# A decoder layer's down-projection: 23 instead of 20 pairs of row blocks in seven products, and second-half weight sums made by accumulating DMAs

## The chip, the cores and the metric

The kernel runs on one core of one Trainium2 chip. The metric is the device time of one execution in microseconds (us), lower is better. The kernel before took 1053.34 us (median of three runs, 1053.02 to 1053.57).

The engines of the core are named as in the profile: PE is TensorE (matmuls; PEld is its weight load), DVE is VectorE, ACT is ScalarE, POOL is GpSimd, SP is the engine that issues nearly all DMAs here. SPq and POOLq are the sequencers that issue them.

## The reference

A hybrid decoder layer on 256 tokens of width 2048, float32 throughout: an input projection, two groups of attention heads, an output projection, and a gated MLP with a causal convolution. The change lies in the MLP:

```python
h = rmsnorm(x, pre_ffn_g[l])
u = causal_dwconv(h @ w_up[l], conv_w[l], conv_b[l])      # w_up: 2048 x 11264
gate, val = jnp.split(u, 2, axis=-1)
y = (jax.nn.gelu(gate, approximate=True) * val) @ w_down[l]   # w_down: 5632 x 2048
x = x + rmsnorm(y, post_ffn_g[l])
```

## The kernel before

**Three matmuls for one.** A float32 product is made from two parts of each operand, a high part rounded to float32r and the remainder (low): high by high, high by low, low by high. For each weight tile ACT writes the high part (`act.copy`, CAST in the profile) and DVE subtracts it from the loaded tile to get the low part (TENSOR_TENSOR). Both parts stand in one of five buffers `wpair`; the loaded tile stands in one of five buffers `raw` of 1024 columns (512 KB). DVE's subtraction is the last reader of a `raw` buffer, and SP may load that buffer again after it; PE's last matmul frees a `wpair`.

**The order of the work.** PE's instructions stand in program order. Those of the other engines are ordered by a scheduler, apart from some that `keep_in_program_order` pins. A counter `tick()` runs once per weight unit of a projection (8 per projection of the MLP, 16 per pair of gate and value projections); `later(n, f)` calls `f` after n such steps.

**The MLP in two halves.** Each half of the 5632 hidden channels is done in two stages. In the `w_up` stage (lines 1002 to 1049) eleven groups `g` of 256 channels each take a gate projection and a value projection (`proj_S`, matmuls of 256 columns on line 300); DVE, ACT and for some sums POOL then make the convolution, the gelu, the product, and the split tiles `G`. In the `w_down` stage (lines 1161 to 1207) the 22 row blocks of that half, taken as 11 pairs, are multiplied by `w_down`, for `n` = 0 and then 2: each time two column blocks of 512 for both blocks of 128 tokens (matmuls of 512 columns on line 1072).

**Four products or seven.** A pair of row blocks against two column blocks is a 2 by 2 block product: eight block products, three matmuls each. `four` does four of them (12 matmuls), for one column block. `seven` does the whole pair in seven products (21 matmuls instead of 24) by a Strassen-Winograd scheme. It needs sums of activation blocks (tiles `s`, `sums`, made by POOL in the `w_up` stage on lines 1030 to 1033, then split by ACT and DVE) and four sums of weight blocks. The weight sums come from one of two places:
- made in the `w_down` stage, by four DVE operations of 512 columns on the loaded tiles (line 1105; the second tile is then called `low`);
- stored beforehand: in the `w_up` stage SP loads the weight blocks (`staged`, line 922), DVE makes the sums (line 928, four operations of 256 columns, twice per pair), SP stores them to DRAM (`t_dram`, line 931). In the `w_down` stage they are loaded as two tiles of 512 KB, the second of them called `two`.

Either way a pair in `seven` splits 3.5 tiles of 1024 columns, and a pair in two calls of `four` splits 2.

`SEVENS` says, for each half and each `n`, at which step `i` of the loop on line 1168 a pair's seven products stand; `STORED` says which pairs' sums are stored beforehand. Each step `i` also holds the products of one pair by `four`: `n` and `n + 1`, except in the last stage (second half, `n` = 2), where `n + 1` comes later. The first half has 6 and 6 pairs in seven products, the second half 5 and 3. After the last seven of an `n`, `fold` (line 1139) adds four PSUM banks into `y_sb`; after the last `four`, `down` (line 1059) adds the other banks.

Buffers that the change touches: `yy` (two of 1024 columns, holding the convolved projections in the `w_up` stage and `low` in the `w_down` stage), `gb0` (one, for `staged` of the second half, for `two`, and later for the gain of the last norm), `gb1` (one, for those activation sums that don't fit in `sums`, named `more`, and later for the gain), `u0` to `u2` (three, the scaled projections ahead of the convolution).

Of the kernel before, what the change touches and what calls it, by code (L numbers as in the profile page):

```python
# [8 lines left out]
F32 = mybir.dt.float32  # L9
# [18 lines left out]
SEVENS = (((0, 0, 1, 1, 2, 2), (0, 0, 1, 1, 2, 2)), ((0, 0, 1, 1, 2), (0, 1, 2)))  # L28
STORED = (((0, 0, 1), (0, 0, 3), (0, 0, 5), (0, 2, 1), (0, 2, 3), (0, 2, 5), (1, 0, 1)), ((1, 0, 3), (1, 2, 0), (1, 2, 1), (1, 2, 2)))
# [5 lines left out]
def hybrid_layer(ctx: ExitStack, tc: tile.TileContext, x, pre_mix_g, w_in, b_forget, sinks,  # L35
# [367 lines left out]


# [448 lines left out]
    with tc.tile_pool(name="ffn", bufs=1) as fp:  # L853
# [22 lines left out]
        NU = 3  # L876
# [3 lines left out]
        fp.tile([P, 8], F32, tag="gap", name="gap")  # L880
# [26 lines left out]
        in_dram = {}  # L907

        def stage(half, n, u, start, step, room):

            k = half * FHALF + u * 2
            t = in_dram[half, n, u] = tc.dram_tile([P, 4, 512], F32, name="t_dram")
            src = w_down[k * P:(k + 2) * P, n * 512:(n + 2) * 512].rearrange(
                "(a p) (b c) -> p a b c", p=P, b=2)
            for i, j in enumerate((slice(0, 256), slice(256, 512))):
# [8 lines left out]
                def add(b=b):  # L924
                    b11, b12, b21, b22 = (b[0][:, i, :] for i in range(4))
                    for y, p, q in ((b11, b12, b11), (b12, b22, b12), (b22, b22, b11),
                                    (b21, b21, b22)):
                        tc.keep_in_program_order(dve.tensor_tensor(y, p, q, op=ALU.subtract))
# [49 lines left out]
        for half in range(2):  # L978
# [5 lines left out]

            def sums_at(u):
                w, at = 384 if u < least else 512, 768 * min(u, least) + 1024 * max(u - least, 0)
                if not u:
                    sums.append(main.tile([P, 4096], F32R, tag="x", name="sums"))
                if at + 2 * w <= 4096:
                    x = sums[0][:, at:at + 2 * w]  # L990
                else:
                    x = fp.tile([P, UNIT], F32R, tag="gb1", name="more")[:, 0:2 * w]
                sums.append((x[:, :w], x[:, w:]))
                return w, *sums[-1]

            for g in range(FHALF // 2):
# [24 lines left out]
                if g < most:  # L1021
# [9 lines left out]
                    pool.tensor_tensor(s1, a21, a22, op=ALU.add)  # L1031
                    pool.tensor_tensor(s2, s1, a11, op=ALU.subtract)
                    pool.tensor_tensor(s4, a12, s2, op=ALU.subtract)
# [6 lines left out]
                if not g:  # L1040
                    if half:
                        room = lambda: fp.tile([P, 4, 256], F32, tag="gb0", name="staged")
                    else:
                        four_of = main.tile([P, 4, 4, 256], F32, tag="y", name="staged")
                        rooms = [four_of[:, i] for i in range(4)]
                        room = lambda: rooms.append(rooms[0]) or rooms.pop(0)
# [37 lines left out]
            def seven(n, u, last, banks, opened):  # L1084
# [8 lines left out]
                else:  # L1093
# [3 lines left out]
                    [x[:, i * P:i * P + P] for x in sums[1 + u]] if i < 3 or u >= least  # L1097
                    else parts_of(u * 2, 1) for i in range(4)]
                (w11,) = split_into(w_parts(UNIT, held=False), top, 1)
                w21, w22 = split_into(w_parts(UNIT, held=False), low, 2)  # L1100
                if t is None:
                    b11, b12, b21, b22 = (x[:, i:i + 512] for x in (top, low) for i in (0, 512))
                    for y, p, q in ((b11, b12, b11), (b12, b22, b12), (b22, b22, b11),
                                    (b21, b21, b22)):
                        made = dve.tensor_tensor(y, p, q, op=ALU.subtract)
# [201 lines left out]
```

## Time and profile before

| | |
|---|---|
| median of three runs | 1053.34 us |
| the profiled execution's own time | 1053.3 us |
| its span, first to last instruction | 1051.4 us |
| mean granted TensorE clock | 0.997 |
| first `w_up` stage of the MLP | about 340 to 577 us of the span |
| first `w_down` stage | 577 to 688.5 us |
| second `w_up` stage | 688.5 to 928 us |
| second `w_down` stage | 928 to about 1044 us |

The page of the profile gives the busy time of each engine and the chain of work that ended last. Matmuls are pipelined and their ends are modelled, so the mean duration of a matmul in a group is longer than its share of the time; its pace is read from the chain, which puts runs of matmuls together. Busy time of an engine that PE doesn't wait for is not time of the kernel.

### The profile page before, as it was taken

To read this page: it belongs to the slowest core of one execution; us is meant where nothing else is said; L and a number is where in the kernel's file an instruction comes from. 1 tells how busy PE (TensorE), PEld (TensorE's weight loads), DVE (VectorE), ACT (ScalarE), POOL (GpSimd) and SP (SyncE) were. 2 spreads that over 40 slices of the span, in tenths; PEclk is the share of its full clock that TensorE was granted. 3 is DMA by queue.
4 is the path that set the end of the run, shared out by engine and by line. 5 is a ranking of instruction groups with operands and counts; after the bars stand their busy time and mean duration, and the time that the engine had idled before them with its cause. 6 is when DMAs were issued, how large, how long until landed. Compare 5 with 4: busy or idle time off the path is not lost.

```text
span 1051.4 us, 19021 instructions
## 1 busy us (share of the span) xinstructions
PE 1040.0 (99%) x7240; PEld 958.0 (91%) x7240; DVE 837.2 (80%) x1365; ACT 626.9 (60%) x1025; POOL 166.5 (16%) x210
## 2 busy tenths in 40 slices
PE   9999999999999999999999999999999999999996
PEld 7899988888888999999999888899999999988886
DVE  5999877887467888888877988967788777799783
ACT  6777757667557655555555655645565455566561
POOL 3253245441122210100000000000111000000023
PEclk9999999999999999999999999999999999999998
DMA  8645557555874878888875886777677776767783
GB/s 292 199 129 168 182 159 214 164 180 171 294 248 153 255 252 294 287 264 273 283 232 170 263 269 226 244 233 239 220 235 246 226 244 219 236 216 246 244 306 115
DMA packets 187335, 238.98 MB, mean 227 GB/s; under 512 B 8268, under 2 KB 154988, under 8 KB 186348
## 3 DMA queue, kind: packets, MB, share of 16 engines
q1 hardware_dynamic: 186924, 237.37, 69.5%
q8 instruction: 57, 0.93, 0.3%
q10 hardware_dynamic: 320, 0.40, 0.1%
q14 instruction: 34, 0.28, 0.1%
HBM read 221.86 MB, written 15.75 MB: 226 GB/s over the span
## 4 chain that ended last, share of the span: by engine, by line
PE 90%; DVE 4%; ACT 2%; DMA 1%; POOL 1%; issue 1%; SPq 0%; DVEq 0%; POOLq 0%; ACTq 0%
PE bank_att L300 23%; PE bank_acc L300 21%; PE bank_acc L1072 15%; PE bank_acc L317 12%; PE bank_acc L263 5%; PE bank_att L1072 5%; PE bank_acc L270 3%; DVE wpair L122 1%; PE bank_att L317 1%; POOL scr L450 1%; PE bank_att L518 1%; DMA raw<-in_w_in_dram 1%; PE bank_att L483 1%; PE bank_att L527 1%; DMA x_in<-in_x_dram 1%
## 5 line engine op out<-in xcount | busy, mean ns | idle before, releaser
L122 DVE TENSOR_TENSOR wpair<-raw,wpair 128x1024 fp32r<-128x1024 f32 (+3 forms) x317 | 383.6, 1225 | 116.9 <-ACT wpair L119 115.8
L119 ACT CAST wpair<-raw 128x1024 fp32r<-128x1024 f32 (+3 forms) x316 | 320.3, 1032 | 155.6 <-issue 62.6
L300 PE MATMUL bank_att<-hT,wpair 128*128 128x256 f32 x2112 | 241.2, 276 | 0.0
L300 PEld LDWEIGHTS bank_att<-hT,wpair 128*128 128x128 f32 x2112 | 240.4, 188 | 0.2
L300 PE MATMUL bank_acc<-hT,wpair 128*128 128x256 f32 x1920 | 219.2, 276 | 0.0
L300 PEld LDWEIGHTS bank_acc<-hT,wpair 128*128 128x128 f32 x1920 | 218.3, 188 | 0.0
L1072 PE MATMUL bank_acc<-wpair,G 128*128 128x512 f32 x636 | 153.5, 389 | 0.0
L1072 PEld LDWEIGHTS bank_acc<-wpair,G 128*128 128x128 f32 x636 | 119.1, 188 | 24.5
L263 PE MATMUL bank_acc<-hT,wpair 128*128 128x512 f32 x384 | 94.9, 394 | 0.0
L263 PEld LDWEIGHTS bank_acc<-hT,wpair 128*128 128x128 f32 x384 | 69.5, 188 | 13.2
L317 PE MATMUL bank_acc<-wpair,oT 128*128 128x512 f32 x336 | 78.0, 391 | 0.0
L317 PEld LDWEIGHTS bank_acc<-wpair,oT 128*128 128x128 f32 x336 | 62.6, 188 | 12.8
L1030 POOL TENSOR_TENSOR s<-yy 128x128 f32<-128x128 f32 x11 | 7.5, 681 | 408.1 <-DVE yy L1019 408.1
L320 ACT CAST wpair<-raw 128x1024 fp32r<-128x1024 f32 (+1 forms) x54 | 48.0, 892 | 36.2 <-PE bank_acc L1072 17.6
L321 DVE TENSOR_TENSOR wpair<-raw,wpair 128x1024 fp32r<-128x1024 f32 (+1 forms) x54 | 55.0, 1023 | 14.3 <-ACT wpair L320 13.4
L899 ACT ACTIVATE yy<-u,cw 128x256 f32<-128x256 f32 x88 | 48.4, 596 | 20.4 <-DVE u L894 15.3
L270 PE MATMUL bank_acc<-hT,wpair 128*128 128x256 f32 x384 | 49.4, 280 | 0.0
L270 PEld LDWEIGHTS bank_acc<-hT,wpair 128*128 128x128 f32 x384 | 47.4, 188 | 1.4
L317 PE MATMUL bank_acc<-wpair,hT 128*128 128x384 f32 (+1 forms) x288 | 47.7, 321 | 0.0
L317 PEld LDWEIGHTS bank_acc<-wpair,hT 128*128 128x128 f32 x288 | 45.4, 188 | 0.1
L320 ACT CAST G<-yy 128x256 fp32r<-128x256 f32 x44 | 16.0, 406 | 46.8 <-POOL yy L1031 23.9
L901 DVE SCALAR_TENSOR_TENSOR yy<-u,cw,yy 128x256 f32<-128x256 f32 x88 | 39.1, 482 | 2.4 <-ACT yy L899 2.2
(253 smaller groups left out, 1204.9 us busy)
## 6 DMA issues: line engine op xcount, KB each, us to landing
raw<-in_w_up_dram SPq DMA_DIRECT2D x176, 512.0 KB, 4.6
raw<-in_w_down_dram SPq DMA_DIRECT2D x68, 512.0 KB, 5.1
raw<-in_w_in_dram SPq DMA_DIRECT2D x51, 512.0 KB, 5.3
raw<-in_w_out_dram SPq DMA_DIRECT2D x32, 512.0 KB, 4.1
staged<-in_w_down_dram SPq DMA_DIRECT2D x44, 256.0 KB, 5.5
t_dram<-staged SPq DMA_DIRECT2D x22, 512.0 KB, 3.2
raw<-t_dram SPq DMA_DIRECT2D x14, 512.0 KB, 3.7
raw<-in_w_in_dram SPq DMA_DIRECT2D x16, 384.0 KB, 3.4
```

The lines of the kernel that those rows point to most:

```text
L119: i1 = act.copy(hi[:, cs], raw[:, cs])
L122: i2 = dve.tensor_tensor(lo[:, cs], raw[:, cs], hi[:, cs].bitcast(F32), op=ALU.subtract)
L263: pe.matmul(b, hi[:, a, m * P:(m + 1) * P], hT[:, kt, 0:512], start=(kt == 0), stop=(last == (0, kt)))
L270: pe.matmul(b[:, 256:512], lo[:, a, m * P:(m + 1) * P], hT[:, u * 4 + a, 0:256], start=False, stop=(last == (1, u * 4 + a)))
L300: pe.matmul(b[:, m * 256:(m + 1) * 256], ws[:, a, m * P:(m + 1) * P], hT[:, kt, i * 256:(i + 1) * 256], start=not begun, stop=last == (low ...
L317: pe.matmul(b, a, r[:, cols], start=(first and i == 0), stop=(last and i == 2))
L320: act.copy(hi, src)
L321: dve.tensor_tensor(lo, src, hi.bitcast(F32), op=ALU.subtract)
L450: pool.tensor_tensor(dst, dst, row, op=ALU.mult)
L899: act.activation(y, u[:, 2:258], AF.Identity, bias=cw[:, 3, ch:ch + 1], scale=cw[:, 2, ch:ch + 1])
L901: dve.scalar_tensor_tensor(y, u[:, 1:257], cw[:, 1, ch:ch + 1], y, op0=ALU.mult, op1=ALU.add)
L1072: pe.matmul(b, x, r, start=b not in opened and not i, stop=closes and i == 2)
```

## The change

The change does seven things:
- `SEVENS`: 7, 7, 6 and 3 pairs in seven products instead of 6, 6, 5 and 3. In the first half the last step that holds sevens (`i` = 2) now holds three of them. In the second half, `n` = 0, it still holds two, and there is one step less.
- `MADE`: in the first `w_up` stage the sums of ten pairs of the first half are made and stored by way of SBUF, where seven pairs were done (one of those seven was of the second half). A half pair now takes 7 steps instead of 10, so that all take 140 steps as before.
- The scheme's signs are turned so that the weight sums need additions alone. In `stage` three DVE operations (one of 512 columns, two of 256) replace four of 256.
- `ADDED`: the seven stored pairs of the second half are no longer made by DVE. SP copies the blocks from DRAM to DRAM (two DMAs of 512 KB), and POOL issues three DMAs that add in place (512, 256 and 256 KB), each 14 steps after the one before; the pairs start 16 steps apart.
- The second tile of stored rows, `two`, is loaded into the two `yy` buffers, not into the one buffer `gb0`.
- Activation sums that don't fit go to `gb1` and `gb2`; `gb2` is new.
- Two buffers `u` instead of three, and `cs` and `last` share the buffer of `s`.

```diff
-SEVENS = (((0, 0, 1, 1, 2, 2), (0, 0, 1, 1, 2, 2)), ((0, 0, 1, 1, 2), (0, 1, 2)))
-STORED = (((0, 0, 1), (0, 0, 3), (0, 0, 5), (0, 2, 1), (0, 2, 3), (0, 2, 5), (1, 0, 1)), ((1, 0, 3), (1, 2, 0), (1, 2, 1), (1, 2, 2)))
+SEVENS = (((0, 0, 1, 1, 2, 2, 2), (0, 0, 1, 1, 2, 2, 2)), ((0, 0, 1, 1, 2, 2), (0, 1, 2)))
+MADE = tuple((0, n, u) for n in (0, 2) for u in (0, 1, 3, 5, 6))
+ADDED = tuple((1, 0, u) for u in (1, 3, 4, 5)) + tuple((1, 2, u) for u in range(3))
...
+        def added(at, start):
+
+            t = in_dram[at] = tc.dram_tile([P, 4, 512], F32, name="t_dram")
+            src = corners(*at)
+
+            def copy():
+                for a in range(2):
+                    tc.keep_in_program_order(sp.dma_start(t[:, 2 * a:2 * a + 2, :], src[:, a]))
+
+            def add(to, what):
+                return lambda: tc.keep_in_program_order(
+                    pool.dma_start(to, what, accum_op=ALU.add))
+
+            for d, f in enumerate((copy, add(t[:, 0:2, :], src[:, :, 1, :]),
+                                   add(t[:, 3, :], t[:, 0, :]), add(t[:, 2, :], t[:, 3, :]))):
+                later(start + d * 14, f)
...
-        NU = 3
+        NU = 2
...
-                    c = fp.tile([P, 256], F32, tag="cs", bufs=1, name="cs")
+                    c = fp.tile([P, 512], F32, tag="s", name="cs")[:, 0:256]
...
                 def add(b=b):
-                    b11, b12, b21, b22 = (b[0][:, i, :] for i in range(4))
-                    for y, p, q in ((b11, b12, b11), (b12, b22, b12), (b22, b22, b11),
-                                    (b21, b21, b22)):
-                        tc.keep_in_program_order(dve.tensor_tensor(y, p, q, op=ALU.subtract))
+                    x = b[0]
+                    for y, p, q in ((x[:, 0:2], x[:, 0:2], x[:, 1:4:2]),
+                                    (x[:, 3], x[:, 3], x[:, 0]), (x[:, 2], x[:, 2], x[:, 3])):
+                        tc.keep_in_program_order(dve.tensor_tensor(y, p, q, op=ALU.add))
...
-                if at + 2 * w <= 4096:
-                    x = sums[0][:, at:at + 2 * w]
+                if sum(x.shape[1] for x in sums) + n > 4096:
+                    x = fp.tile([P, UNIT], F32R, tag=f"gb{len(places)}", name="more")
...
-                    for at in STORED[half]:
-                        start = stage(*at, start, 19 if half else 10, room)
+                    for at in MADE:
+                        start = stage(at, start, 7, lambda: rooms.append(rooms[0]) or rooms.pop(0))
+                if half and not g:
+                    for i, at in enumerate(ADDED):
+                        added(at, 1 + i * 16)
...
-                        own = None if tail else fp.tile([P, UNIT], F32, tag="gb0", name="two")
+                        own = None if tail else fp.tile([P, UNIT], F32, tag="yy", bufs=2, name="two")
```

How instructions move, at three places. First, VectorE at the end of the first half's `n` = 0. Before, from the last pair in sevens to the last `down` (`wpair` rows are splits, L1145 to L1148 the fold, L1061 `down`; names after the arrow are inputs):

```order
L321 TENSOR_TENSOR wpair<-two,wpair 128x1024
L122 TENSOR_TENSOR wpair<-raw,wpair 128x1024 x3
L1145 TENSOR_TENSOR y_sb<-bank_att,y_sb 128x512
L122 TENSOR_TENSOR wpair<-raw,wpair 128x1024
L1146 TENSOR_TENSOR y_sb<-bank_att,y_sb 128x512
L1147 TENSOR_TENSOR y_sb<-bank_att,y_sb 128x512
L321 TENSOR_TENSOR wpair<-raw,wpair 128x512
L1148 TENSOR_TENSOR y_sb<-bank_att,y_sb 128x512
L321 TENSOR_TENSOR wpair<-low,wpair 128x1024
L122 TENSOR_TENSOR wpair<-raw,wpair 128x1024
L1061 TENSOR_TENSOR y_sb<-bank_acc,y_sb 128x512 x2
```

The same place in the changed kernel (L1174 to L1177 are the fold, L1090 is `down`):

```order
L322 TENSOR_TENSOR wpair<-two,wpair 128x1024
L123 TENSOR_TENSOR wpair<-raw,wpair 128x1024 x2
L322 TENSOR_TENSOR wpair<-raw,wpair 128x512
L1174 TENSOR_TENSOR y_sb<-bank_att,y_sb 128x512
L322 TENSOR_TENSOR wpair<-raw,wpair 128x1024
L1175 TENSOR_TENSOR y_sb<-bank_att,y_sb 128x512
L1176 TENSOR_TENSOR y_sb<-bank_att,y_sb 128x512
L1090 TENSOR_TENSOR y_sb<-bank_acc,y_sb 128x512
L1177 TENSOR_TENSOR y_sb<-bank_att,y_sb 128x512
L123 TENSOR_TENSOR wpair<-raw,wpair 128x1024
L1090 TENSOR_TENSOR y_sb<-bank_acc,y_sb 128x512 x3
```

One pair by `four` less stands between the sevens and the next `n`, so that the fold and all of `down` come within two splits of each other.

Second, SyncE's queue at the same place, from the last two pairs in sevens on. Before (`raw` of 512 columns and of 1024 columns are a stored pair's untouched blocks, `two` and `raw<-t_dram` its sums):

```order
L74 DMA raw<-in_w_down_dram 128x512
L74 DMA raw<-in_w_down_dram 128x1024
L74 DMA two<-t_dram 128x1024
L74 DMA raw<-t_dram 128x1024
L74 DMA raw<-in_w_down_dram 128x2x512 x2
L74 DMA low<-in_w_down_dram 128x1024
L74 DMA raw<-in_w_down_dram 128x2x512 x2
```

In the changed kernel:

```order
L75 DMA raw<-in_w_down_dram 128x512
L75 DMA raw<-in_w_down_dram 128x1024
L75 DMA two<-t_dram 128x1024
L75 DMA raw<-t_dram 128x1024
L75 DMA raw<-in_w_down_dram 128x512
L75 DMA raw<-in_w_down_dram 128x1024
L75 DMA two<-t_dram 128x1024
L75 DMA raw<-t_dram 128x1024
L75 DMA raw<-in_w_down_dram 128x2x512 x2
```

Two stored pairs now follow each other, where one was followed by loads for `four`.

Third, GpSimd's queue in the second `w_up` stage, at its third and fourth group. Before it held only the activation sums:

```order
L1030 TENSOR_TENSOR s<-yy 128x128
L1031 TENSOR_TENSOR yy<-yy 128x128
L1032 TENSOR_TENSOR s<-yy 128x128
L1033 TENSOR_TENSOR s<-yy,s 128x128
L1030 TENSOR_TENSOR s<-yy 128x128
L1031 TENSOR_TENSOR s<-yy 128x128
L1032 TENSOR_TENSOR s<-s,yy 128x128
```

In the changed kernel the adding DMAs stand between them:

```order
L1060 TENSOR_TENSOR s<-yy 128x128
L1061 TENSOR_TENSOR yy<-yy 128x128
L1062 TENSOR_TENSOR s<-yy 128x128
L1063 TENSOR_TENSOR s<-yy,s 128x128
L424 DMA t_dram<-t_dram 128x512 x2
L424 DMA t_dram<-in_w_down_dram 128x2x512
L1060 TENSOR_TENSOR s<-yy 128x128
```

From the fourth group on, a group's four sums stand behind three adding DMAs of three different pairs.

More of the change, by code (lines that the diff above doesn't have):

```diff
@@ L402, in hybrid_layer, with corners @@
             unit_T(parts, u, bq0)
+        in_dram = {}
+        def corners(half, n, u):
+            k = half * FHALF + u * 2
+            return w_down[k * P:(k + 2) * P, n * 512:(n + 2) * 512].rearrange(
+                "(a p) (b c) -> p a b c", p=P, b=2)
+        def added(at, start):
[10 more added lines that the diff above has]
+                later(start + d * 14, f)
         gst = const.tile([32, P], F32, tag="gpre", name="gst")
@@ L879, in hybrid_layer @@
             pool.memset(u[:, :, 0:2], 0.0)
-        fp.tile([P, 8], F32, tag="gap", name="gap")
+        fp.tile([P, 16], F32, tag="gap", name="gap")
         cnt = [0]
@@ L905, in conv, with stage @@
             return y
[L907 to L914, printed above, removed]
+        def stage(at, start, step, room):
+            t = in_dram[at] = tc.dram_tile([P, 4, 512], F32, name="t_dram")
+            src = corners(*at)
             for i, j in enumerate((slice(0, 256), slice(256, 512))):
@@ L983, in hybrid_layer, with sums_of @@
             sums = []
+            places = []
             def sums_at(u):
-                w, at = 384 if u < least else 512, 768 * min(u, least) + 1024 * max(u - least, 0)
+                n = 768 if u < least else 1024
                 if not u:
-                    sums.append(main.tile([P, 4096], F32R, tag="x", name="sums"))
-                if at + 2 * w <= 4096:
-                    x = sums[0][:, at:at + 2 * w]
-                else:
-                    x = fp.tile([P, UNIT], F32R, tag="gb1", name="more")[:, 0:2 * w]
-                sums.append((x[:, :w], x[:, w:]))
-                return w, *sums[-1]
+                    places.append(main.tile([P, 4096], F32R, tag="x", name="sums"))
+                if sum(x.shape[1] for x in sums) + n > 4096:
+                    x = fp.tile([P, UNIT], F32R, tag=f"gb{len(places)}", name="more")
+                    places.append(x)
+                    x = x[:, 0:n]
+                else:
+                    at = sum(x.shape[1] for x in sums)
+                    x = places[0][:, at:at + n]
+                sums.append(x)
+                return n // 2, x[:, :n // 2], x[:, n // 2:]
+            def sums_of(u, i):
+                w = sums[u].shape[1] // 2
+                return [sums[u][:, j * w + i * P:j * w + i * P + P] for j in range(2)]
             for g in range(FHALF // 2):
@@ L1039, in hybrid_layer @@
                     split(*parts, s[:, :w])
[L1040 to L1046, printed above, removed]
-                    start = 0
-                    for at in STORED[half]:
-                        start = stage(*at, start, 19 if half else 10, room)
+                if not half and not g:
+                    four_of = main.tile([P, 4, 4, 256], F32, tag="y", name="staged")
+                    rooms = [four_of[:, i] for i in range(4)]
+                    start = 0
+                    for at in MADE:
[3 more added lines that the diff above has]
+                        added(at, 1 + i * 16)
             if half == 1:
@@ L1096, in seven @@
                 s2, s3, s4, s1 = [
-                    [x[:, i * P:i * P + P] for x in sums[1 + u]] if i < 3 or u >= least
-                    else parts_of(u * 2, 1) for i in range(4)]
+                    sums_of(u, i) if i < 3 or u >= least else parts_of(u * 2, 1)
+                    for i in range(4)]
                 (w11,) = split_into(w_parts(UNIT, held=False), top, 1)
@@ L1102, in seven @@
                     b11, b12, b21, b22 = (x[:, i:i + 512] for x in (top, low) for i in (0, 512))
-                    for y, p, q in ((b11, b12, b11), (b12, b22, b12), (b22, b22, b11),
+                    for y, p, q in ((b11, b11, b12), (b12, b12, b22), (b22, b22, b11),
                                     (b21, b21, b22)):
-                        made = dve.tensor_tensor(y, p, q, op=ALU.subtract)
+                        made = dve.tensor_tensor(y, p, q, op=ALU.add)
                         if n and not u and y is b11:
@@ L1264, in hybrid_layer @@
             finish(0, slice(n * 512, (n + 1) * 512), r, sp)
-        last = fp.tile([P, 256], F32, tag="cs", bufs=1, name="last")
+        last = fp.tile([P, 512], F32, tag="s", name="last")[:, 0:256]
         for h in range(2):
```

12 lines of the change are left out of this document (6 added, 6 removed).

## Prediction

> **What bounds the kernel now.** I read the page first, then the chain that ended last, then stretches of the stages that the change touches.
>
> ```profile
> span 1051.4 us, 19021 instructions
> PE 1040.0 (99%) x7240; PEld 958.0 (91%) x7240; DVE 837.2 (80%) x1365; ACT 626.9 (60%) x1025; POOL 166.5 (16%) x210
> PE 90%; DVE 4%; ACT 2%; DMA 1%; POOL 1%; issue 1%; SPq 0%; DVEq 0%; POOLq 0%; ACTq 0%
> ```
>
> The profiled execution took 1053.3 us, 1.9 us around its span of 1051.4; it lies 0.04 us from the median of 1053.34. I sum against 1053.3. PE holds 90% of the chain, and the question is whether it ever pauses where the change works. The chain, in order of time (start, duration, instructions):
>
> ```profile
> 359.35 21.79 PE bank_att L300 x192
> 381.14 21.76 PE bank_acc L300 x192
> ...
> 555.22 21.76 PE bank_acc L300 x192
> ...
> 607.60 6.80 PE bank_acc L1072 x30
> 614.40 2.04 PE bank_att L1072 x9
> ...
> 621.20 11.56 PE bank_acc L1072 x51
> ...
> 1034.48 8.64 PE bank_att L317 x72
> 1044.55 0.75 DVE y_sb L1233
> ```
>
> Each run of 192 matmuls of 256 columns takes 21.76 us, 113.3 ns each, and the next begins where it ends. In `w_down` 30 matmuls of 512 columns take 6.80 us, 9 take 2.04, 51 take 11.56: always 226.7 ns. From 359 to 1043 us PE has no gap to speak of. So the change can gain only by the matmuls that it removes, and loses whatever makes PE wait. DVE, DMA and POOL matter only as suppliers. The same by stretches (busy us of PE, PEld, DVE, ACT, POOL with counts, then PE clock, DMA share, GB/s):
>
> ```profile
> 381.10:402.90 21.80, 21.80 (x195) 21.80 (x194) 19.42 (x33) 12.02 (x17) 2.43 (x4) 1.00 0.96 305
> 389.00:409.00 20.00, 20.00 (x179) 20.00 (x178) 17.25 (x28) 11.61 (x17) 1.24 (x3) 1.00 1.00 332
> 486.00:496.00 10.00, 10.00 (x90) 10.00 (x89) 8.92 (x16) 5.71 (x9) 0.00 (x0) 1.00 1.07 372
> 577.00:632.80 55.80, 55.80 (x247) 46.19 (x247) 50.11 (x59) 34.84 (x39) 0.00 (x0) 1.00 0.80 266
> 753.80:775.50 21.70, 21.70 (x194) 21.70 (x193) 17.53 (x28) 12.21 (x17) 2.03 (x4) 1.00 0.70 221
> ```
>
> PE stays busy even where the DMA share is 1.00 over 20 us at 332 GB/s, and 1.07 over 10 us at 372.
>
> **The matmuls removed.** A pair by seven is 7 x 3 = 21 matmuls of 512 columns, by `four` twice 24. The first half goes from 6 x 21 + 5 x 24 = 246 (246 x 0.2267 = 55.8 us, the stretch 577.0 to 632.8) to 7 x 21 + 4 x 24 = 243, for each of two `n`. The second half's `n` = 0 goes from 5 x 21 + 6 x 24 = 249 to 246; the last stage keeps its 3. Nine matmuls go: 9 x 0.2267 = **2.04 us**. Everything else is off PE.
>
> **VectorE in the first `w_up` stage.** Group rows (line, form, count; busy, mean ns), then one tile's operations (min/median/max ns):
>
> ```profile
> L928 DVE TENSOR_TENSOR staged<-staged 128x256 f32<-128x256 f32 x88 | 37.8, 430 | 1.6
> L321 DVE TENSOR_TENSOR wpair<-low,wpair 128x1024 fp32r<-128x1024 f32 x18 | 22.0, 1221 | 1.3 <-ACT wpair L320 0.9
> L1061 DVE TENSOR_TENSOR y_sb<-bank_acc,y_sb 128x512 f32<-128x512 f32 x15 | 9.7, 682 | 6.4 <-PE bank_acc L1072 6.4
> L1105 DVE TENSOR_TENSOR low<-low x9: 681/686/695, 576.0 to 959.9; 128x512 f32<-128x512 f32 x9
> ```
>
> Seven pairs cost 7 x 8 x 0.430 = 24.1 us. Ten cost 10 x 2 x (0.686 + 2 x 0.430) = 30.9 us, +6.8 us over 140 steps of 1.36 us (21.76 / 16). In a stretch of 21.8 us that is 3.5 us for 2.8, so DVE at its busiest goes from 19.42 to some 20.2 of 21.8. It is hidden by the 2.4 us of idle time there; without that cover it would be PE's loss, at most 0.8 us a group. Counted at nothing. The second `w_up` stage loses 32 x 0.430 = 13.8 us of DVE, which PE doesn't wait for.
>
> **DMA in the first `w_up` stage.** Issues by line (count, KB each, us to landing):
>
> ```profile
> raw<-in_w_up_dram SPq DMA_DIRECT2D x176, 512.0 KB, 4.6
> staged<-in_w_down_dram SPq DMA_DIRECT2D x44, 256.0 KB, 5.5
> t_dram<-staged SPq DMA_DIRECT2D x22, 512.0 KB, 3.2
> two<-t_dram SPq DMA_DIRECT2D x8, 512.0 KB, 6.2
> ```
>
> Eight loads of `w_up` in 21.76 us are 193 GB/s. The 11 stored pairs take 44 loads and 22 stores, so one moves 1 MB in and 1 MB out, 2.1 MB: seven in 190 us are 77 GB/s, ten are 110. The stretch at 305 GB/s would ask for 338, a mean one for 303 to 312. Held against 332 over 20 us and 372 over 10 us with PE unbroken, it passes, with landings later than 4.6 us. The cover is five `raw` buffers of 2.72 us each (24 matmuls), 13.6 us. If 332 were a hard limit, the densest group would lose 338 / 332, 0.4 us. Counted at nothing.
>
> **The `w_down` stages.** For the first half's last two steps of an `n` (three sevens, two pairs by `four`, the fold, `down`) PE has 111 matmuls, 25.2 us. DVE has 3 x (0.68 + 3 x 1.22) = 13.0 for sevens, 4 x 1.22 = 4.9 for `four`, 4 x 0.69 = 2.7 for the one pair made in place, 4 x 0.68 for the fold and as much for `down`: 26.1 us, 0.9 more than PE. Before, the last three steps had 24.2 us in 25.8. But busy times overlap at their ends, as merged rows show (start, duration, count):
>
> ```profile
> 963.42 2.35 DVE L122 TENSOR_TENSOR wpair<-raw,wpair 128x1024 fp32r<-128x1024 f32 x2
> 629.59 1.28 DVE L1061 TENSOR_TENSOR y_sb<-bank_acc,y_sb 128x512 f32<-128x512 f32 x2
> ```
>
> Two splits take 2.35, so they follow at 1.13 us, and two `down` at 0.60. By these the sum is 3 x 4.0 + 4 x 1.13 + 12 x 0.60 = 23.7 us, 1.5 less than PE has. The cost per `n` lies between 0 and 0.9 us; I take 0, since the second reckoning is the one by start times. The earlier steps of an `n` lose two in-place pairs (i = 0 now has none), so DVE enters them less loaded.
>
> SP's queue there:
>
> ```profile
> 616.89 1.23 DVE L321 TENSOR_TENSOR wpair<-two,wpair 128x1024 fp32r<-128x1024 f32 x1
> 618.14 0.34 SPq L74 DMA_DIRECT2D two<-t_dram  x1
> 620.80 1.05 ACT L119 CAST wpair<-raw 128x1024 fp32r<-128x1024 f32 x1 [1.16 <-DMA raw<-in_w_down_dram]
> ```
>
> With one buffer, `two` waits until DVE has read the one before (618.12), and the `raw` loads queued behind it on SP make ACT wait 1.16 us for one. PE didn't notice, as the chain shows. Two buffers move that wait to the reader of two tiles ago, which takes this stall away; next late are the loads of two stored pairs in a row, 3.5 MB in 9.5 us (42 matmuls), with three `raw` loads per 4.76 us against a landing of 3.2 to 6.2. No gain, no cost.
>
> **POOL and DMA in the second `w_up` stage.** Seven pairs bring 14 SP copies of 512 KB and 21 adds on POOL. The copies wait for nothing. An add waits for the DMA before it in its pair; behind it on POOL stand the next group's activation sums, and for these ACT waits already:
>
> ```profile
> ACT G L320 <- POOL yy L1031: 23.9, 9, 3.5
> POOL s L1030 <- DVE yy L1019: 408.1, 11, 239.0
> ```
>
> POOL is busy 2.03 of 21.7 us in the stretch from 753.8, so it idles some 19 us a group ahead of its sums, and each add was preceded by its source a group (16 steps, 21.76 us) or 14 steps earlier. Landings are 3.2 to 6.2 us, so the waits are over before POOL comes to them: 0. No row shows an adding DMA. A bound from below is a copy of its size (5.5 us, its engines' time at 1 x); from above I take three times that, 17 us, still under 21.76. The adds' data per pair is 1.05 MB, as are the copies', so in a group of 21.76 us they ask 48 + 48 GB/s beside 193, in all 289, less than the first stage. Counted at nothing; nearest are the loads and stores of 3.2 to 6.2 us.
>
> Two `u` buffers: a buffer is written again 21.76 us after its last writing, and its readers follow within a group: 0. The gain's early load, 512 KB, and the shared `cs`: 0.
>
> **Sum.** 1053.3 - 2.04 = **1051.3 us**.
>
> **The rivals.** 0.2% (2.1 us) is about what a measurement of this kernel can tell from no change; the bounds are 1051.2 and 1055.4, and my sum lies 0.1 us inside the first.
>
> *VectorE late at the end of an `n`.* The upper reckoning holds: up to 0.9 us twice in the first half, and the new `raw` pinch as much again: 1051.6 to 1053.3. For it speaks 26.1 against 25.2; against it the start times. 0.18.
>
> *Slower matmuls.* Every `G` tile moves in SBUF, and here matmuls of one shape have two paces:
>
> ```profile
> 355.69 3.66 PE bank_acc L263 x16
> ```
>
> 16 of 512 columns in 3.66 us are 228.8 ns, 2.1 over those of `w_down`. On the 243 + 243 + 246 that remain in the changed parts that would cost 1.5 us: 1052.8. Against it, nothing ties the pace to an address. 0.05.
>
> *Slower: the DMA engines bound the second `w_up` stage.* If an add keeps them k times as long as a copy, they are asked for 193 + 48 + 48k GB/s. From 332, k = 1.9, PE starts to wait; over the 152 us of the seven pairs k = 2.2 makes 347 / 332, +7 us, and 1058; k = 3 makes +24. For it: adds read two sources. Against it: 372 GB/s over 10 us, and a slow queue would delay itself before it delays `raw`, whose cover is 13.6 us. 0.10. The Trainium skill ("Collectives: The Full Stack", section "The bandwidth ceiling: the fold count and why AG ≠ RS ≠ AR") holds that a reducing DMA is slowed not by its addition but by reading two sources, to about half a copy's rate. By that rule k is 2, as an estimate 337 GB/s, +2.3 us and 1053.6; no run here shows an add yet.
>
> *Slower: POOL's queue.* If a pair's add takes over 21.76 us, POOL waits, ACT's split of `G` waits for the sums, and the weight casts behind it on ACT starve PE: five groups of (X - 21.8), at X = 25 us +16. 0.03.
>
> **How the numbers follow.** My forecast 0.62, the rivals 0.18, 0.05, 0.10 and 0.03, the rest 0.02. Runs of before spread by 0.3 us around the median, so the forecast falls beyond 1051.2 in four of ten cases: faster 0.62 x 0.42 + 0.01 = 0.27. Slower: most of the DMA rival, POOL's, and a rest: 0.12. Same: 0.61. Likeliest 1051.3; the range from 1050.9 (0.4 us of scatter) to 1053.4 holds the forecast, late VectorE and slower matmuls, 0.85, less scatter.
>
> **What would show it.** Right: 243, 243 and 246 matmuls at 226.7 ns, the first `w_down` stage ending 1.4 us and the second 2.0 us sooner, `w_up` groups still at 21.76 us. Wrong: groups over 21.76 us in the second `w_up` stage with a DMA share near 1 (DMA) or a long wait of ACT's `G` on POOL (queue); a gap of PE at the change of `n` with DVE without idle time ahead of it (VectorE); runs of 30 over 6.80 us (pace).

## The result, and the profile after

The changed kernel takes **1063.24 us** (median of 4 runs, 1061.99 to 1063.76) where the kernel before takes 1053.34: a ratio of 1.0092, 95% interval 1.0075 to 1.011. It is slower by 9.9 us; the forecast was 1051.3, in a range of 1050.9 to 1053.4.

The head of the changed kernel's page: span, busy times, the two DMA queues that matter (packets, MB, share of the engines' time), and the chain's shares.

```profile
span 1062.0 us, 19079 instructions
PE 1043.7 (98%) x7231; PEld 958.5 (90%) x7231; DVE 830.2 (78%) x1333; ACT 628.9 (59%) x1033; POOL 193.3 (18%) x238
q1 hardware_dynamic: 187756, 247.33, 71.7%
q0 software_dynamic: 3920, 7.34, 5.1%
PE 73%; DMA 9%; DVE 8%; ACT 3%; issue 3%; POOL 2%; SPq 0%; DVEq 0%; ACTq 0%; POOLq 0%
```

PE has its nine matmuls fewer (7231 for 7240), but its share of the chain fell from 90% to 73%, and DMA's rose from 1% to 9%. The chain in order of time shows where. The first `w_up` stage is as before, the second is not:

```profile
359.94 21.79 PE bank_att L301 x192
...
555.80 21.76 PE bank_acc L301 x192
```

```profile
733.72 21.76 PE bank_att L301 x192
...
766.12 12.98 DMA raw<-in_w_up_dram
...
847.64 14.29 DMA raw<-in_w_up_dram
...
869.21 21.76 PE bank_att L301 x192
...
942.63 7.54 DMA low<-in_w_down_dram
950.27 1.05 ACT wpair L321
951.35 1.23 DVE wpair L322
952.63 7.58 PE bank_acc L1101 x25
```

In the second `w_up` stage the chain runs through loads of `w_up` that land 13 to 14 us after their issue (median before: 4.6), and in the second `w_down` stage through a load of `low`. The last line shows a second cost: 25 matmuls at 226.7 ns are 5.67 us, and these took 7.58.

The starts of the matmuls give an account by stage. What a stage lost is the time from its first matmul to the next stage's (in the second `w_down` stage to its last matmul of 512 columns), less its matmuls at 113.33 ns (256 columns) or 226.7 ns (512). Three of the kernels made below, numbered by their experiments, stand beside. The rows of losses are of one profiled execution each (1053.3, 1063.8, 1055.4, 1063.8 and 1053.2 us), the last row is the median of all runs:

| us | before | changed | adds left out (2) | ring eased, adds kept (13) | both undone (9) |
|---|---|---|---|---|---|
| first `w_up`, lost | 0.0 | 0.0 | 0.0 | 0.0 | 0.0 |
| first `w_down`, lost | 0.0 | 2.4 | 2.2 | 0.5 | 0.8 |
| second `w_up`, lost | 0.0 | 5.0 | 0.0 | 11.3 | 0.0 |
| second `w_down`, lost | 0.3 | 4.4 | 1.8 | 0.6 | 0.3 |
| time, median | 1053.3 | 1063.2 | 1055.4 | 1062.7 | 1052.0 |

For the changed kernel 11.8 - 0.3 lost and 2.0 gained make 9.5 of the 10.6 us by which the spans differ; the rest lies ahead of the first `w_up` stage (0.6) and behind the last matmul (0.5), where nothing was changed.

Three places make these losses. **One:** the second `w_up` stage while the adds run (busy us and counts of PE, PEld, DVE, ACT, POOL, then PE clock, DMA share, GB/s):

```profile
690.00:755.00 65.00, 65.00 (x575) 64.99 (x574) 47.22 (x65) 35.01 (x46) 7.36 (x11) 1.00 0.93 271
755.00:865.00 110.00, 107.33 (x930) 106.94 (x929) 75.03 (x107) 54.98 (x77) 26.77 (x33) 0.98 1.01 262
```

The same stretch before:

```profile
755.00:865.00 110.00, 110.00 (x973) 110.00 (x972) 86.86 (x132) 61.72 (x85) 8.04 (x12) 1.00 0.73 232
```

The DMA engines are full (1.01) at only 262 GB/s; before, a share of 1.00 went with 332 GB/s (20 us of the first `w_up` stage). The transfers of this stage, by queue and issue (KB each, us to landing):

```profile
q1 hardware_dynamic: 41157, 47.21, 66.0%
q0 software_dynamic: 3920, 7.34, 24.8%
...
raw<-in_w_up_dram SPq DMA_DIRECT2D x72, 512.0 KB, 6.4
t_dram<-in_w_down_dram SPq DMA_DIRECT2D x12, 512.0 KB, 6.3
t_dram<-in_w_down_dram POOLq DMA_DIRECT2D x7, 512.0 KB, 11.5
t_dram<-t_dram POOLq DMA_DIRECT2D x14, 256.0 KB, 6.5
```

Over these 219 us (712 to 931) queue 0, which holds the adds alone, took 24.8% = 54.3 us for 7.34 MB; queue 1, SyncE's loads and copies, took 144.5 for 47.21. Per MB that is 7.4 against 3.06, a factor k of 2.4. The wait that this brings is ACT's, for tiles of `w_up` (total, times, longest; the kernel before has no such wait):

```profile
ACT wpair L120 <- DMA raw<-in_w_up_dram: 29.5, 18, 6.3
```

**Two:** the ring, as the two buffers of the tag `yy` are called from here on, which `yy`, `low` and `two` take in turn; here at the start of the second `w_down` stage:

```profile
937.86 1.22 DVE L322 TENSOR_TENSOR wpair<-low,wpair 128x1024 fp32r<-128x1024 f32 x1
939.10 0.33 SPq L75 DMA_DIRECT2D two<-t_dram  x1
...
941.85 0.75 DVE L322 TENSOR_TENSOR G<-yy,G 128x256 fp32r<-128x256 f32 x2
942.63 0.33 SPq L75 DMA_DIRECT2D low<-in_w_down_dram  x1
...
950.27 1.04 ACT L321 CAST wpair<-low 128x1024 fp32r<-128x1024 f32 x1 [4.38 <-DMA low<-in_w_down_dram]
```

The same place before:

```profile
930.54 1.22 DVE L321 TENSOR_TENSOR wpair<-low,wpair 128x1024 fp32r<-128x1024 f32 x1
931.78 0.33 SPq L74 DMA_DIRECT2D low<-in_w_down_dram  x1
```

Before, the slot that the first `low` leaves goes to the next `low`, 4.0 us into the stage. Now `two` takes it, and `low` has to wait for the other slot, until VectorE has split the last `yy`: 8.3 us into the stage. It lands 7.5 us later, and PE stands still.

**Three:** the change of `n` in the first half, where PE waits for a bank that VectorE's `down` (line 1090) hasn't emptied:

```profile
634.28 1.21 DVE L123 TENSOR_TENSOR wpair<-raw,wpair 128x1024 fp32r<-128x1024 f32 x1
...
635.41 1.88 DVE L1090 TENSOR_TENSOR y_sb<-bank_acc,y_sb 128x512 f32<-128x512 f32 x3
...
636.15 0.96 PE L1101 MATMUL bank_acc<-wpair,sums 128*128 128x512 f32 x3 [0.84 <-DVE y_sb L1090]
```

### The profile page after: what moved, and what is told of

The parts are those of the page before. It is cut to its first block, busy times and chain, and to the rows that moved or that the text cites. A ratio compares the mean times of both kernels' runs of the same rounds, so it can differ in the third digit from the quotient of the medians.

```text
span 1062.0 us, 19079 instructions
## 1 busy us (share of the span) xinstructions
PE 1043.7 (98%) x7231; PEld 958.5 (90%) x7231; DVE 830.2 (78%) x1333; ACT 628.9 (59%) x1033; POOL 193.3 (18%) x238
## 3 DMA queue, kind: packets, MB, share of 16 engines
q0 software_dynamic: 3920, 7.34, 5.1%
## 4 chain that ended last, share of the span: by engine, by line
PE 73%; DMA 9%; DVE 8%; ACT 3%; issue 3%; POOL 2%; SPq 0%; DVEq 0%; ACTq 0%; POOLq 0%
PE bank_att L301 17%; PE bank_acc L301 16%; PE bank_acc L318 12%; PE bank_acc L1101 11%; PE bank_acc L264 5%; DMA raw<-in_w_up_dram 5%; PE bank_att L1101 4%; DVE wpair L123 3%; PE bank_acc L271 3%; DMA low<-in_w_down_dram 2%; ACT wpair L120 1%; DMA raw<-t_dram 1%; PE bank_att L318 1%; POOL scr L475 1%; PE bank_att L543 1%
## 5 line engine op out<-in xcount | busy, mean ns | idle before, releaser
L123 DVE TENSOR_TENSOR wpair<-raw,wpair 128x1024 fp32r<-128x1024 f32 (+3 forms) x311 | 376.1, 1225 | 120.2 <-ACT wpair L120 118.7
L120 ACT CAST wpair<-raw 128x1024 fp32r<-128x1024 f32 (+3 forms) x310 | 311.8, 1031 | 125.6 <-DMA raw<-in_w_up_dram 29.5
L1101 PE MATMUL bank_acc<-wpair,G 128*128 128x512 f32 x582 | 144.7, 392 | 2.3 <-ACT wpair L321 1.2
L1101 PEld LDWEIGHTS bank_acc<-wpair,G 128*128 128x128 f32 x582 | 109.3, 189 | 26.9 <-DVE wpair L322 1.8
L322 DVE TENSOR_TENSOR wpair<-raw,wpair 128x1024 fp32r<-128x1024 f32 (+1 forms) x66 | 67.5, 1034 | 19.2 <-ACT wpair L321 18.9
L321 ACT CAST wpair<-raw 128x1024 fp32r<-128x1024 f32 (+1 forms) x66 | 59.0, 901 | 38.0 <-PE bank_acc L1101 13.5
```

The lines of the kernel that those rows point to most:

```text
L120: i1 = act.copy(hi[:, cs], raw[:, cs])
L123: i2 = dve.tensor_tensor(lo[:, cs], raw[:, cs], hi[:, cs].bitcast(F32), op=ALU.subtract)
L321: act.copy(hi, src)
L322: dve.tensor_tensor(lo, src, hi.bitcast(F32), op=ALU.subtract)
L1101: pe.matmul(b, x, r, start=b not in opened and not i, stop=closes and i == 2)
```

## The experiments

Theory: two separate things make the loss, the accumulation of the adds (engine time, so late loads of `w_up`) and `two` in the ring (so a late `low`). Rivals: the adds' path and not the accumulation (copies from DRAM to DRAM, SyncE's queue, GpSimd's descriptors); a backlog of transfers and not the ring; the new order of the pairs.

**1. The ring undone: `two` in its own single buffer.**

```
- own = None if tail else fp.tile([P, UNIT], F32, tag="yy", bufs=2, name="two")
+ own = None if tail else fp.tile([P, UNIT], F32, tag="gb0", name="two")
```

> The changed kernel with one line undone: `two` gets its own single buffer back and leaves the ring of two that `yy` and `low` share. Theory (ring): in the changed kernel `two` takes the slot that the next pair's `low` would have had, so `low` is issued later by about 4 to 11 us, lands late, and PE waits; here the late `low` goes, the first w_down stage loses 1.1 us instead of 2.4, the second 0.3 instead of 4.4, and the time is 1057.7. Rival 1 (backlog: `low` lands late because transfers of the stage before are still under way): within 0.5 us of the changed kernel, 1062.7 to 1063.7. Rival 2 (one buffer is too few where two stored pairs follow each other): `low` is in time, but `two` is late instead, and 1 to 3 us come back in each n with such pairs: 1060 to 1063.

1068.87 us (1065.58 to 1072.21). In the second `w_down` stage PE no longer waited for `low`, as the theory says; the stage still lost 1.9, 1.2 of it in one wait for ACT near its end. But the first lost 7.4: rival 2, and more than it gave. Where two stored pairs follow each other, `two` is loaded only when the one before has been read:

```profile
683.79 1.04 ACT L321 CAST wpair<-two 128x1024 fp32r<-128x1024 f32 x1 [4.78 <-DMA two<-t_dram]
...
684.88 0.50 PE L1101 MATMUL bank_att<-wpair,more 128*128 128x512 f32 x1 [0.85 <-ACT wpair L321]
```

So the change couldn't have kept one buffer: a second one was needed, and the ring was the wrong place for it. The second `w_up` stage lost 8.2 here, 3 more than in the changed kernel, with the same adds; why isn't shown.

**2. The adds left out.**

```
  def add(to, what):
-     return lambda: tc.keep_in_program_order(pool.dma_start(to, what, accum_op=ALU.add))
+     return lambda: None
```

> The changed kernel without its 21 accumulating DMAs; the 14 copies into the stored pairs of the second half stay, so these pairs hold rows of w_down in place of their sums. Theory (the adds keep the DMA engines longer per byte than a copy): the second w_up stage goes from 244.3 to 239.4 us, everything else stays, 1058.3. Rival (the copies from DRAM to DRAM, or SyncE's queue behind them, delay the loads): at least half of the 5 us stays, 1060.7 or more.

1055.44 us: 7.8 less than the changed kernel, more than the 5 expected. The second `w_up` stage lost nothing:

```profile
755.00:865.00 110.00, 110.00 (x973) 110.00 (x973) 81.64 (x117) 62.47 (x86) 11.04 (x16) 1.00 0.73 232
```

The rest of the 7.8 went in the second `w_down` stage (1.8 lost in place of 4.4). There `low` is issued as late as in the changed kernel (8.4 us into the stage against 8.3), but it lands in 6.0 us in place of 7.5, and the slow stretch behind the wait (1.4 us, see below) doesn't come. What made `low` land later in the changed kernel isn't shown: the last adds were issued 75 us earlier. The copies are harmless.

**3. The adds as plain copies on the same queue.**

```
-     pool.dma_start(to, what, accum_op=ALU.add)
+     pool.dma_start(to, what)
```

> The changed kernel with the 21 accumulating DMAs of GpSimd as plain copies of the same source to the same place, so the stored pairs of the second half are no sums. It tells apart why they are slow. If it is the accumulation (reading two sources): their landings fall from 11.5 us (512 KB) and 6.5 (256 KB) towards the copies' 6.3 and below, the second w_up stage takes 239.4, 1058.3. If it is GpSimd's queue or the way its descriptors are made: as the changed kernel, 244 and 1063.

1055.86 us, the second `w_up` stage lost nothing. Its transfers over the same stage:

```profile
q0 software_dynamic: 2128, 7.34, 15.5%
...
raw<-in_w_up_dram SPq DMA_DIRECT2D x72, 512.0 KB, 4.8
...
t_dram<-in_w_down_dram POOLq DMA_DIRECT2D x7, 512.0 KB, 8.0
t_dram<-t_dram POOLq DMA_DIRECT2D x14, 256.0 KB, 6.5
```

The same bytes on the same queue took 33.9 us of the engines in place of 54.3, and the loads of `w_up` land in 4.8 again. So it is the accumulation, not GpSimd's queue: GpSimd waited for landings here too (20.2 us in 5 waits, 23.6 in 5 in the changed kernel). One thing changes with the accumulation, as the rows of queue 0 show: the adds went as 3920 packets, the plain copies as 2128 for the same bytes. Per packet, the adds kept an engine no longer (54.3 us x 16 / 3920 = 222 ns against 255). Whether the accumulation costs by reading a second source or by its smaller packets isn't told apart here.

**4. Three sevens in the first step** (and `two` alone in its buffer).

```
- SEVENS = (((0, 0, 1, 1, 2, 2, 2), (0, 0, 1, 1, 2, 2, 2)), ...
+ SEVENS = (((0, 0, 0, 1, 1, 2, 2), (0, 0, 0, 1, 1, 2, 2)), ...
- MADE ... for u in (0, 1, 3, 5, 6)
+ MADE ... for u in (0, 1, 2, 4, 6)
```

> The kernel with `two` in its own buffer, and the first half's sevens as 3, 2, 2 per step in place of 2, 2, 3 (the two pairs made in place stay the first ones of the last two steps). Theory (VectorE late at the change of n, since three sevens, the fold and `down` fall together): the wait of 1.1 us at the change of n goes, 1.1 us less than the kernel with `two` alone, 1056.6 if that gives 1057.7. Rival (VectorE is late by the fold and `down` alone): the same time as that kernel. A third way: three sevens at the start want more rows at once than arrive, and 1 us or more is lost there.

1067.92 us, with waits for `two` at the start of an `n` as in 1, so the times can't be compared. The wait at the change of `n` didn't go: VectorE's `down` was late by 1.3 us even with two sevens in the last step. That speaks against three sevens as its cause.

**5. The ring alone, in the kernel before.** The line of experiment 1, the other way.

> The kernel before with one line of the change: `two` shares the ring of two with `yy` and `low`. Theory (ring): `low` of the next pair made in place is issued later, and PE waits for it in both w_down stages, 1 to 3 us in the first and 0.5 to 4 in the second: 1055 to 1060. Rival (the new order of the pairs, not the ring, makes `low` late): 1053.3 within 0.5 us.

1056.80 us, ratio 1.0032 (1.0021 to 1.0043): +3.3 from one line. The profiled execution was the fastest (1055.14); it lost 0.8 in the first `w_down` stage and 1.2 more than before in the second. The chain shows the same pattern as the changed kernel's, in the first `w_down` stage:

```profile
583.81 0.42 DVE G L321
...
584.25 6.10 DMA low<-in_w_down_dram
```

`low` starts when the last `yy` has been split (before: at 580.73). The new order of the pairs isn't needed for it.

**6. The adds further apart.**

```
- added(at, 1 + i * 16)
+ added(at, 1 + i * 19)
```

> The changed kernel with 19 steps in place of 16 between one added pair and the next. By the queue rows of the changed kernel the adds keep the DMA engines 54.2 us and seven copies of 1.05 MB at 325 GB/s 22.6 us, beside loads of w_up that ask 193 of 325 GB/s, 59%. At 16 steps (152.3 us) that is 110% of the engines, at 19 steps (180.9 us) 102%. Theory (the engines' total time): the second w_up stage loses 0 to 2 us in place of 5, 1058 to 1060. Rival (each pair's adds hold the loads up by themselves, however far apart): the loss stays at 5 us, 1063.

1060.48 us (1056.53 to 1061.13), 2.8 less than the changed kernel. But the profiled execution, the slowest (1061.13), didn't save this where the theory has it: its second `w_up` stage still lost 4.9, and the saving lies in the second `w_down` stage (2.3 lost in place of 4.4) and in the first (2.0 for 2.4). The 4.9 are another mixture: PE's waits for weights came later (from 869 us on, in place of 827) and made 2.7 us, and behind them the matmuls kept a slower pace to the end of the stage:

```profile
888.75 22.61 PE bank_acc L301 x192
```

So this run doesn't decide between the theories: the median lies just above the first one's range, the profiled stage fits the second. The runs spread over 4.6 us, and no profile shows what the one of 1056.53 did.

**7. Four added pairs, 36 steps apart, in the plan of the kernel before** (its `SEVENS`, its stored pairs, `two` in its own buffer).

```
- ADDED = tuple((1, 0, u) for u in (1, 3, 4, 5)) + tuple((1, 2, u) for u in range(3))
+ ADDED = ((1, 0, 3), (1, 2, 0), (1, 2, 1), (1, 2, 2))
- added(at, 1 + i * 16)
+ added(at, 1 + i * 36)
```

> The plan of the kernel before (6 and 6, 5 and 3 pairs in seven, the pairs that it stored, `two` in its own buffer), but with its four pairs of the second stage made by copies and accumulating DMAs, 36 steps apart. By the same rows these ask 22% of the DMA engines' time beside 59%. Theory (the engines' total time): the second w_up stage takes 239.4 us, and the kernel 1053.3, as before. Rival (each pair's adds hold the loads up by themselves): four sevenths of the 5 to 8 us, 1056 to 1058.

1053.65 us, ratio 1.0001 (0.9992 to 1.0011), no stage lost anything:

```profile
755.00:865.00 110.00, 110.00 (x973) 110.00 (x972) 81.50 (x116) 62.15 (x85) 17.15 (x22) 1.00 0.86 246
```

At a share of 0.86 the adds are hidden, though each is still slow (512 KB in 9.4 us, 11.5 in the changed kernel). So a single pair's adds don't hurt. Fewer pairs and wider gaps go together here: that it is the engines' total time, and not how many adds run at once, fits this run and isn't shown apart.

**8. No adds, and a ring half eased: VectorE makes the seven pairs, and every other `two` leaves the ring.**

```
- def stage(at, start, step, room):
+ def stage(at, start, step, room, then=(4, 16)):
- for i, at in enumerate(ADDED):
-     added(at, 1 + i * 16)
+ start = 0
+ for at in ADDED:
+     start = stage(at, start, 11, lambda: fp.tile(
+         [P, 4, 256], F32, tag="gb0", name="staged"), (5, 7))
- own = None if tail else fp.tile([P, UNIT], F32, tag="yy", bufs=2, name="two")
+ twos[0] += 1
+ own = fp.tile([P, UNIT], F32, name="two", **(
+     dict(tag="gb0") if twos[0] % 2 else dict(tag="yy", bufs=2)))
```

> The changed kernel with two edits: the seven pairs of the second stage are made by VectorE through one buffer (load, sums, store, 11 steps each half), without accumulating DMAs, and every other `two` gets the buffer of its own, so that the ring is entered half as often. Theory: the second w_up stage takes 239.4 us, the first w_down stage loses 1 us in place of 2.4, the second 0.3 in place of 4.4: 1052.3, 1 us below the kernel before. Rival (VectorE, with seven pairs more in the second w_up stage, is late there): 1 us or more per group with pairs, 1058 or more. A third way: half the entries into the ring are as bad as all, 2.2 and 1.7 us stay as without adds, 1055.2.

1053.28 us, ratio 0.9996 (0.9987 to 1.0005). Second `w_up` and second `w_down` lost nothing beyond the kernel before; the first `w_down` lost 1.9, 0.9 of it for a `low` near 592 us.

**9. The same, with the other `two` in the ring in the first half** (the count starts anew in each `w_down` stage).

```
+ twos[0] = 1 - half
```

> The kernel with VectorE's sums and every other `two` in the buffer of its own, but in the first w_down stage the first, third, ... `two` go into the ring and the others into that buffer (the second stage as it was). Theory (the late `low` of the first n, 0.7 us of waiting in two places near 592 us, comes of the `two` that took its slot just before): these waits go, 0.9 us less, 1052.4. Rival (the ring has an entry too many whichever comes first): the wait stays or moves to the next `low`, 1053.3 or more.

**1052.02 us**, ratio 0.9988 (0.9979 to 0.9997): faster than both kernels, 1.3 us below the kernel before. The interval only just leaves out no change, and it is the best of the five kernels of 8 to 12. Its profiled execution is its slowest, 1053.24; 1.0 of that lies ahead of the first `w_up` stage. Ahead of the change of `n` the first `w_down` stage is clean (whole runs of 6.80 and 2.04), and what is left of its loss, 0.8, is that change:

```profile
629.50 1.23 DVE L322 TENSOR_TENSOR wpair<-raw,wpair 128x1024 fp32r<-128x1024 f32 x1 [1.59 <-ACT wpair L321]
...
634.17 1.88 DVE L1094 TENSOR_TENSOR y_sb<-bank_acc,y_sb 128x512 f32<-128x512 f32 x3
...
634.91 0.96 PE L1105 MATMUL bank_acc<-wpair,sums 128*128 128x512 f32 x3 [0.49 <-DVE y_sb L1094]
```

VectorE is late with `down` although it stood idle for 1.59 us five us earlier, behind a cast that waited for a late `raw`.

**10. The last pair of an `n` made in place** (on top of 9): `MADE` with `u` in (0, 1, 3, 5) in place of (0, 1, 3, 5, 6).

> As the kernel with the other `two` first, but the last pair by seven of each n of the first half is made in place by VectorE and no longer stored: 2.7 us more of VectorE's work in the last step of an n, 0.8 MB less to load there. It tells apart the wait of PE at the change of n (0.8 us near 634 us). Theory 1 (VectorE has too much work there): the wait grows to 1.5 to 3.5 us, 1053 to 1055. Theory 2 (VectorE is late because rows of stored pairs land late and it idles 1.6 us for them): the wait falls to 0.3 us or less, 0.5 us less than that kernel.

1053.11 us, ratio 1.0004 (0.9986 to 1.0021). With 2.7 us more of VectorE's work there the three `down` began at 631.69, in 9 at 634.17: the wait for the bank went, as theory 2 says. But a wait of 1.1 us for a split of weights came in its place, so the time says nothing for either. The three `down` also stand ahead of a split here that came before them in 9, which may have helped them. Two of its ten runs took 1062.1 and 1062.5; one is the profiled one, and its whole second `w_up` stage, with no wait, ran at the slower pace seen in 6:

```profile
689.27 22.61 PE bank_att L301 x192
```

Its clock was 1.00, and the DMA engines had room:

```profile
690.00:755.00 65.00, 65.00 (x554) 65.00 (x553) 51.39 (x72) 33.69 (x45) 5.24 (x8) 1.00 0.79 255
```

**11. Three sevens in the middle step** (on top of 9): `SEVENS` (0, 0, 1, 1, 1, 2, 2) for both `n`, `MADE` with `u` in (0, 1, 3, 4, 6).

> As the kernel with the other `two` first, but the first half's sevens are 2, 3, 2 per step in place of 2, 2, 3, and the pairs made in place are again the first of the last two steps. If three sevens beside the fold and `down` are what makes VectorE late at the change of n, the wait of 0.8 us near 634 us goes: 0.5 to 0.8 us less than that kernel. If it is the loads, it stays, or a wait of 1 us or more comes in the middle step, where three sevens want their rows.

1053.05 us, ratio 0.9996 (0.9987 to 1.0005); the wait for `down` stayed (0.8). With 4 this settles that three sevens in the last step aren't its cause; whether VectorE's load or late rows are stays open, with the idle time in 9 and the early `down` in 10 for the rows.

**12. The second half alone changed** (on top of 9): first half of the kernel before.

> The first half as in the kernel before (6 and 6 pairs, three stored in each n, `two` in its own buffer), the second half as changed (6 pairs in seven in its n = 0) with its seven stored pairs made by VectorE and every other `two` in the ring. Three matmuls of 512 columns fewer, 0.7 us: the first w_down stage takes 111.5 us, the second w_up stage 239.4, the second w_down stage loses 0.3 us: 1052.8. Rival: the second w_down stage loses a wait for `low` again, 1 to 2 us: 1054 to 1055.

1052.60 us, ratio 0.9993 (0.9984 to 1.0002). Every stage as expected; the three matmuls are worth 0.7 by count and 0.8 by the medians, though the interval doesn't leave out 0.

**13. The ring eased, the adds kept.** The changed kernel with the lines on `twos` of 8 and 9 alone.

> The changed kernel, its 21 accumulating DMAs kept, with only the ring eased: in each w_down stage every other `two` gets the buffer of its own (as in the kernel with VectorE's sums that took 1052.0). Its losses in the changed kernel were 2.4 us in the first w_down stage, 5.0 in the second w_up, 4.2 in the second w_down. Theory (the second w_down stage's 4.2 us are the ring's alone): it loses nothing there, 0.8 in the first, the adds' loss in the second w_up stays: 1063.2 - 1.6 - 4.2 = 1057.4. Rival (the adds' after-effect makes 2.6 of the 4.2, the part that was gone without adds): 2 us or more stay in the second w_down stage, 1059.5 or more.

1062.69 us: the time was missed by 5 us. The second `w_down` stage lost 0.6, only 0.3 more than before and none of it for `low`, and the first lost 0.5. So what the changed kernel lost in the second `w_down` stage needs the ring; how much of it comes depends on how soon `low` lands, as 2 shows (1.8 with the whole ring and no adds). But the second `w_up` stage, with the same adds, now lost 11.3:

```profile
PE bank_att L301 <- DVE wpair L123: 3.0, 1, 3.0
PE bank_acc L301 <- DVE wpair L123: 1.4, 1, 1.4
```

```profile
870.60 22.61 PE bank_att L301 x192
...
915.83 22.61 PE bank_att L301 x192
```

Waits make 5.3 of it, matmuls at half pace, most of them behind the longest wait, 1.7, and the slower pace, four runs of 192 at 22.6 us and part of a fifth, 4.0. Against 9, where VectorE makes the same pairs (1052.02), this kernel is 10.7 us slower. The slower pace came without adds too (10), so its 4.0 us aren't shown to be the adds'.

## Why the prediction was wrong

**The matmuls: right.** 243, 243 and 246 in place of 246, 246 and 249, and where PE doesn't wait, runs of 30 still take 6.80 us (9). **The first `w_up` stage: right**, with ten stored pairs and VectorE's three adds a chunk: the runs of 192 at 21.76 are unbroken.

**The step that failed first: "adds bounded 5.5 to 17 us ... counted at nothing".** A bound on one add's landing was used where the engines' time counts. An add of 512 KB did land in 11.5 us, inside the bound, and POOL's queue never mattered (3 has the same queue and no loss). The rival "the DMA engines bound the second `w_up` stage" had the mechanism, from k = 1.9 on, and got 0.10. Measured, k is 2.4 against SyncE's loads and copies. By that rival's own sum 193 + 48 + 48 x 2.4 = 356 GB/s against 332 over 152 us gives +11. The profile of the changed kernel shows 5.0 in this stage; that of 13 shows 11.3, but with 4.0 of the slower pace in it, so that its nearness to 11 is luck. What spoke against it in the prediction was false: the slow adds delayed SyncE's loads too, from a median of 4.6 us to 6.4 (4.8 with plain copies), and some `raw`, with a cover of 13.6 us, landed after 13 to 14. The Trainium skill ("Collectives: The Full Stack", section "The bandwidth ceiling: the fold count and why AG ≠ RS ≠ AR") has the reducing step of a collective's ring at half the rate of its copying step. The direction holds here, and the two factors measured lie on either side of it: 2.4 against SyncE's loads and copies, 1.6 against plain copies on the adds' own queue.

**The step that failed second: "with one buffer, `two` waits ... two buffers move that wait ... no gain, no cost".** It asked how long `two` waits, and not whose buffers the two are. The diff says `tag="yy"`, which is `low`'s ring: 14 more entries delay `low`, which PE needs at once. Alone it costs 3.3 us (5); in the changed kernel 3.8 in the second `w_down` stage (4.4 against 0.6 in 13) and about 1.6 in the first (2.4 against 0.8 in 9). Half the entries, the right half, cost nothing (9).

**VectorE late at the change of `n`: the rival was right in place and size** (0.8 to 1.1 us, and only at the first of the two). That three sevens in the last step make it is refuted (4, 11); the cause stays open.

**Left out altogether: what a wait of PE costs beyond itself.** The prediction took a wait's length as its price. In the changed kernel a wait of 2.7 us at 826.8 was followed by 16 matmuls at 213 ns each, and 2.4 us of waiting at 950 by 7 at 427 ns; by stretches, with the clock as the last column but two:

```profile
829.70:833.10 3.40, 3.40 (x17) 3.40 (x18) 3.40 (x7) 1.09 (x2) 0.00 (x0) 0.53 1.04 348
...
952.70:956.10 3.40, 3.40 (x9) 2.63 (x10) 3.40 (x5) 1.56 (x2) 0.00 (x0) 0.51 0.20 61
960.00:963.40 3.40, 3.40 (x16) 2.81 (x16) 1.93 (x2) 1.94 (x2) 0.00 (x0) 1.00 0.80 207
```

The granted clock is 0.53 and 0.51 behind the waits and 1.00 elsewhere, for 3.4 to 3.7 us each time: 1.6 and 1.4 us on top of 2.7 and 2.4. The Trainium skill ("TensorE: Matmul & The Clock Gate", section "What's actually happening") has the array at half clock after an idle window of about 3.4 us and until as long a busy one. The length of the slow stretch agrees; here shorter waits sufficed, in 1 even two of 1.0 us each within 2.3 us, while a wait of 2.9 us in the same run was not followed by one. The stretches behind the two, from 1:

```profile
838.20:841.60 3.40, 3.40 (x30) 3.40 (x31) 3.40 (x7) 1.09 (x2) 0.00 (x0) 1.00 1.03 354
686.80:690.20 3.40, 3.40 (x10) 2.65 (x9) 3.40 (x4) 3.24 (x4) 0.00 (x0) 0.53 0.47 138
```

**The sum.** Adds 7.8 (2, with the ring in place), ring 3.0 (9 against 2, by their stages, without adds), change of `n` 0.8, matmuls -2.0: 9.6, against 9.9 measured. With the ring eased the kernel with adds is 10.7 slower than that without (13 against 9). Adds and ring don't simply add up, and the same adds went with 5.0, 8.2, 10.4 and 11.3 us lost in the second `w_up` stage (changed, 1, 4, 13). In 4 and 13 the slower pace makes 4.4 and 4.0 of that; what makes the rest of the difference isn't shown.

## What to carry to other kernels

Cost a new kind of DMA by the time it keeps the shared engines, per byte, and add it to what the stage already asks; its own landing time says nothing about the loads beside it. Where an edit moves a tile to another tag, list everything that rotates through that tag and ask which entry PE needs next. A wait of PE of some 2 us or more can cost one and a half times its length.

## What the runs showed of the hardware

- Accumulating DMAs within DRAM took 2.4 times the engines' time per byte of SyncE's loads and copies and 1.6 times that of plain copies on their own queue (54.3 and 33.9 us for 7.34 MB), in 1.8 times as many packets (3920 and 2128). They were hidden at a DMA share of 0.86 and not at 1.01.
- After waits of 2.0 to 2.7 us PE ran at half clock for about 3.5 us, but not after one of 2.9; what decides it wasn't tried.
- The same matmuls of 256 columns have two paces, 192 in 21.76 or in 22.61 us (113.3 or 117.8 ns). The slower one set in behind waits (6, 13) and once at the start of a stage without a wait (10), and lasted to the end of the stage. It isn't the granted clock (1.00 in both). Over a whole stage it cost 9.4 us (10), nearly as much as the whole change; its cause is open.
